# Norms of q and k in a decoder step: one square, one sum by head and one scaling per part, in two of three head groups

## The chip, the cores and the metric

The kernel runs on one core of a Trainium2 chip. The metric is the device time of one execution in microseconds (us), the median of three runs where several were made. A core has five engines that run at the same time, each working through its own list of instructions in order: TensorE (PE, with its weight loads shown as PEld) for matrix products, VectorE (DVE), ScalarE (ACT) and GpSimd (POOL) for elementwise work, and SyncE (SP), which issues transfers between device memory (DRAM) and the on-chip memory SBUF. PE writes its products to a small second memory, PSUM, from which DVE and ACT read. An instruction that needs another engine's result waits on a semaphore, and everything behind it on its own engine waits too.

## The reference, cut to what matters

One step of a decoder layer is computed for 1024 prompt tokens and 64 sample tokens (8 sequences of 8), width 1024. The part that the change touches is the norm of queries and keys: each of 12 heads of 64 channels, for q and for k, is divided by the root of its mean square over the token.

```python
def rms_norm(x, w):
    x32 = x.astype(F32)
    y = x32 * lax.rsqrt(jnp.mean(jnp.square(x32), axis=-1, keepdims=True) + EPS)
    return y.astype(x.dtype) * w

def project(x, ln1, w_in, q_norm, k_norm):
    p = jnp.einsum('btd,de->bte', rms_norm(x, ln1), w_in)
    a, q, k, v, g_a, g_b = jnp.split(p, IN_SPLITS, axis=-1)
    heads = lambda t: t.reshape(B, T, N_HEADS, HEAD_DIM)
    return a, rms_norm(heads(q), q_norm), rms_norm(heads(k), k_norm), heads(v), g_a, g_b
```

The heads form three groups of four. Each group attends over a window with its own stride: (128, 1), (512, 4), (2048, 16). The groups' outputs are combined by their softmax denominators, multiplied with gates and a pooling branch, and followed by an output projection and a feed-forward layer of width 4096. All of it is float32.

## The kernel before

**Order of the stages.** The pooling inputs come first (to about 60 us of the profiled execution), then the three head groups in the order 2, 1, 0 (to about 390 us, group 2 ending near 160), then the gates (tiles `pg`), the mixing and output projection (`pab`, `ph`), the feed-forward layer up (`pz`) and down (`pd`). Matrix products are made in three passes over high and low parts of both operands: `split` (lines 116 and 117) rounds a raw tile to its high part on ACT and subtracts to get the low part on DVE. The weights of q, k and v of one group lie in three rotating places (`places`), loaded through three raw buffers (`raw_qkv`) in pieces of 512 columns; SP issues a load when DVE's line 117 has freed a raw buffer.

**Parts.** In each group, `qkv_part` (line 605) runs for nine blocks of tokens: eight of 128 prompt tokens, and block 8 with the 64 sample tokens. For blocks 1 to 5, q and k are one part of 512 columns (a wide part, PSUM tile `pqk`) and v another of 256; for blocks 8, 0, 6 and 7, q, k and v are three parts of 256 (tiles `pq`, `pk`, `pv`; narrow parts). `js` lists what a part holds (0 for q, 1 for k, 2 for v) and is sorted by the place in which each weight lies. The places of q, k and v are 2, 0 and 1 in every group (`place[0]` is 2, 5 and 8 when a group takes them), so a wide part's `js` is [1, 0]: k in the first 256 columns of the tile, q in the others.

**The norm of one part.** After the matrix products of a q or k part, ACT squares each head's 64 columns from PSUM into the tile `qk` as scratch and accumulates their sum into one column of `ms` (line 642; the profile shows the square and an accumulator read). POOL adds epsilon (line 645) and raises to the power -1/2 (line 646, tile `mr`). Later, at the next step, `scale` multiplies each head's 64 columns from PSUM with its column of `mr` into `qk` on ACT (line 651). For a wide part these are 8 squares, 8 accumulator reads and 8 scalings.

**What follows a part.** Attention of a block is a generator that is advanced one step per part: PE transposes `qk` (line 667, tiles `tqg..`), ACT and DVE copy the result out (`qkT`, lines 669 and 670), PE makes scores (line 684, `sg..`), DVE adds the mask and takes the row extreme (line 693, `smg..` and `sta` or `md`), ACT takes exponentials (line 694), PE transposes them (line 703, `tpg..`), ACT copies that out (line 706, `pTg..`) and PE multiplies with v (line 717, `pog..`). Group 0 needs its tokens in natural order, so during a block's v part the next block's activations are cast into `natt` (line 601; the low halves on ACT, the high halves on DVE). The sample's own keys of group 2 run alongside groups 1 and 0: POOL multiplies loaded cache pieces (line 851, `pck` and `pcv`), DVE reduces or adds them (lines 864, 889, 890). `behind_pe` adds a wait on the most recent matrix product to an instruction; POOL's products of that loop also wait for the last norm on POOL (`last_norm`).

**Who sets the order.** PE's list is written out by hand: it runs in the order of the program. The lists of DVE, ACT, POOL and SP are ordered by a planner, which simulates the program with estimated durations and picks by priority whatever can start. The order is then fixed, whatever the real durations are.

Of the kernel before, what the change touches and what calls it, by code (L numbers as in the profile page):

```python
# [9 lines left out]
AF = mybir.ActivationFunctionType  # L10
ALU = mybir.AluOpType
AX = mybir.AxisListType
# [15 lines left out]
HD = 64  # L28
KPC = 4
H = TOK // 2  # L30
# [7 lines left out]
def decoder_step(ctx, tc, i, o):  # L38
    nc = tc.nc
    v_, s_, g_, t_ = nc.vector, nc.scalar, nc.gpsimd, nc.tensor  # L40
# [8 lines left out]
    def rr(p, shape, dt, name, tag, bufs):  # L49

        n = turn[p, tag] = turn.get((p, tag), -1) + 1
        return p.tile(shape, dt, name=name, tag=f"{tag}.{n % bufs}", bufs=1)
# [133 lines left out]
    def behind_pe(ins, mm=None):  # L186

        tc.add_manual_dep(ins.ins, (mm or last_mm[0]).ins.name,
                          mybir.DependencyInfo(mybir.DependencyClass.Sync, mybir.DependencyReason.DATA), reason="pace")

    def gemm(out, n_k, lhs, rhs, by_k=False, middle=None, quarter=None):

        if by_k == 2:
            terms = [(a, b, k) for k in range(n_k) for a, b in PASSES]
        elif by_k:
            terms = [(1, 0, k) for k in range(n_k)] + [(0, b, k) for k in range(n_k) for b in range(2)]
        else:
            terms = [(a, b, k) for a, b in PASSES for k in range(n_k)]
        for j, (a, b, k) in enumerate(terms):
            last_mm[0] = t_.matmul(out, lhs(a, k), rhs(b, k), start=(j == 0), stop=(j == len(terms) - 1))  # L200
            if middle and j == len(terms) // 2 - 1:
                middle()
            if quarter and j % 6 == 5:
                quarter(j // 6)
# [26 lines left out]
    def bank(name):  # L231
        held[0] = (held[0] + 1) % 4
        return acc_p.tile([P, 512], F32, name=name, tag=f"acc.{held[0]}", bufs=1)
# [212 lines left out]
    def soon(*fs):  # L446

        if fs:
            later.append(lambda: (fs[0](), soon(*fs[1:])))
# [108 lines left out]
    def step():  # L558
        for f in [later.pop(0) for _ in range(len(later))]:
            f()  # L560
        for r in list(active):
            if next(r, True):
                active.remove(r)
        cool[0] -= 1
        for r in waiting[:2]:
            if r not in primed:
                primed.add(r)
                next(r)
        if waiting and cool[0] <= 0:
            r = waiting.pop(0)  # L570
            if not next(r, True):
                active.append(r)
            cool[0] = 2
# [7 lines left out]
    def block_cols(g, blk, s, k):  # L581


        if g == 0:
            return nat[s, k]
        if g == 1:
            return act4[s][k][:, blk // 2, blk % 2 * P:(blk % 2 + 1) * P]
        return act4[s][k][:, blk // 2, blk % 2:2 * P:2]

    def res8(blk):  # L590
        return blk // 2 + 4 * (blk % 2)
# [4 lines left out]
    def in_order(blk, ks=range(0, KD, 2)):  # L596

        for s, copy in ((1, s_.copy), (0, v_.tensor_copy)):
            for k in ks:
                t = natt[:, 4 * s + k // 2]  # L600
                copy(t.rearrange("p k (l r) -> p k l r", r=4),
                     act_t[s].rearrange("p k (r l) -> p k l r", r=4)[:, k:k + 2, blk * 32:(blk + 1) * 32, :].bitcast(F32))
                nat[s, k], nat[s, k + 1] = t[:, 0, :], t[:, 1, :]

    def qkv_part(g, wts, blk, name, tiles, js, middle=None, quarter=None):


        n = min(P, TOK - blk * P)
        qk, vt = tiles
        go = 0 if blk == 8 else g  # L610
        col = res8(blk) if go == 2 else blk
        pt = bank(f"p{''.join('qkv'[j] for j in js)}{name}")
        js = sorted(js, key=lambda j: wts[j])
        N = 256 * len(js)
        at = places[:, wts[js[0]]:wts[js[-1]] + 1:max(1, wts[js[-1]] - wts[js[0]])]

        def rhs(s, k):
            return at[:, :, s, k * 256:(k + 1) * 256]

        if blk == 8:  # L620
            for k in range(KD):
                t_.matmul(pt[:, :N], smp_t[:, k, :], rhs(0, k), start=(k == 0), stop=(k == KD - 1))
                if k < KD - 1:
                    for kk in ((0, 1) if k == 0 else (k + 1,)):
                        last_mm[0] = t_.matmul(pt[:n, :N], smp_t[:, kk, :NS], rhs(1, kk), start=False, stop=False)
            v_.tensor_copy(vt[:n], pt[n:, :256])
            v_.tensor_tensor(pt[:n, :256], pt[:n, :256], vt[:n], op=ALU.add)
        else:
            by_k = 2 if quarter or js == [2] and (g == 0 or blk == 0) else g == 0
            gemm(pt[:n, :N], KD, lambda s, k: block_cols(g, blk, s, k), rhs, by_k, middle, quarter)  # L630
        for j in js:
            ends_of[g, blk, j] = last_mm[0]
        if blk < 8:
            if g == 0 and 2 in js and blk < 7:
                in_order(blk + 1)
        if js[0] < 2:
            ms = rr(ap1, [P, 8], F32, name=f"ms{name}_{js[0]}", tag="ms", bufs=4)
            r = rr(ap1, [P, 8], F32, name=f"mr{name}_{js[0]}", tag="mr", bufs=4)
            H = 4 * len(js)
            for u, j in enumerate(js):  # L640
                for h in range(4):
                    s_.activation(qk[:n, j * 256 + h * HD:j * 256 + (h + 1) * HD],
                                  pt[:n, u * 256 + h * HD:u * 256 + (h + 1) * HD], AF.Square,
                                  scale=HD ** -0.5, accum_out=ms[:n, 4 * u + h:4 * u + h + 1])
            g_.tensor_tensor(ms[:n, :H], ms[:n, :H], xeps[go][:n, col:col + 1].to_broadcast([n, H]), op=ALU.add)
            last_norm[0] = g_.tensor_tensor(r[:n, :H], ms[:n, :H], mhalf[:n, :H], op=ALU.pow)  # L646

            def scale():
                for u, j in enumerate(js):
                    for h in range(4):  # L650
                        behind_pe(s_.activation(qk[:n, j * 256 + h * HD:j * 256 + (h + 1) * HD],
                                                pt[:n, u * 256 + h * HD:u * 256 + (h + 1) * HD], AF.Copy,
                                                scale=r[:n, 4 * u + h:4 * u + h + 1]))
                    if j and blk == 8:
                        v_.tensor_tensor(qk[:n, 256:], qk[:n, 256:], wrow[:n], op=ALU.mult)
                        soon(lambda: sample_keys_out(g, qk))
        else:
            s_.activation(vt[:n], pt[:n, :256], AF.Copy, scale=rtok[go][:n, col:col + 1])
        step()
        if js[0] < 2:  # L660
            soon(scale)
# [446 lines left out]
    def sample_keys_out(g, qk):  # L1108
        rows, new = sample_rows_of(g)
        behind_pe(dma_st(rows[:, :256], qk[:64, 256:]))  # L1110
        if g == 2:
            behind_pe(dma_st(new[:, :512], qk[:64]))
# [23 lines left out]
    for g in (2, 1, 0):  # L1136
# [42 lines left out]
        for blks in ((8, 0), (1,), (2,), (3,), (4,), (5,)) + (((6, 7),) if g else ((6,), (7,))):  # L1179
# [12 lines left out]
            for js in (((0, 1), (2,)) if blks[0] in (1, 2, 3, 4, 5) else ((0,), (1,), (2,))):  # L1192
                for b in (blks[::-1] if g < 2 and js == (2,) and 8 in blks else blks):
# [13 lines left out]
                    if g == 1 and extra and (1, "keys") in done:  # L1207
                        extra = []
                        natt = np_.tile([P, 8, 2, P], F32R, name="natt", tag="nat")
                        soon(lambda: in_order(0, (0, 2)), lambda: in_order(0, (4, 6)))  # L1210
                    wide = len(js) == 2
                    qkv_part(g, wts, b, f"{g}_{b}", tiles[b], js, middle if wide else None,
                             quarter if g and b in (6, 7) else None)
                    feed()
# [139 lines left out]
    def row_tile(n, name):  # L1354
        return rr(rows_p, [P, H], F32, name=f"g{n}_{name}", tag=f"g{n}", bufs=2)
# [149 lines left out]
    for n, (f, a) in enumerate(order):  # L1505
# [5 lines left out]
        t = row_tile(1 + a, f)  # L1511
# [194 lines left out]
    for j in range(2):  # L1706
        for d in range(4):
# [4 lines left out]
            for m in range(2):  # L1712
# [19 lines left out]
                else:  # L1732
                    sq = rr(hq_p, [P, H], F32, name=f"hq{kk}_{j}", tag="hq", bufs=2)
# [478 lines left out]
```

## Time and profile before

| what | us |
|---|---|
| median of three runs (lowest, highest) | 1407.88 (1403.77, 1408.54) |
| profiled execution, its own time | 1405.47 |
| its span, first to last instruction | 1403.7 |
| DVE busy in the span | 965.2 |
| ACT busy in the span | 758.0 |
| POOL busy in the span | 234.2 |
| POOL's step `mr` (line 646), mean of 8 columns (15 times) | 1.77 |
| POOL's step `mr` (line 646), mean of 4 columns on 128 rows (18 times) | 1.11 |
| ACT's scaling of 64 columns from `pqk` (line 651), mean | 0.333 |
| ACT's square of 64 columns from `pqk` (line 642), mean | 0.232 |

All times are from one profiled execution except the first row. In the rows of the profile, the name before the arrow is the tile written, those behind it the tiles read; a shape is partitions by elements. In rows of a group, the number behind "x" counts instructions, then come busy time and mean duration in ns, then the idle time of that engine just before them with what ended most of it. In a timeline row the first two numbers are start and length in us, and the bracket holds the idle time before it and its releaser. In rows of waits, the three numbers are the total in us, how often, and the longest. A row of a stage gives its borders, its length and the busy time of PE, PEld, DVE, ACT and POOL, with the granted clock, the DMA share and GB/s last. The core's granted TensorE clock is 1.000 over the whole span.

### The profile page before, as it was taken

The numbers are of one execution on the slowest core, as the hardware profiler recorded it, in microseconds if no ns is written. First come the engines' busy times: TensorE is split into PE (matmuls) and PEld (weight loads), VectorE is DVE, ScalarE is ACT, GpSimd is POOL, SyncE is SP. The second block draws the span as 40 slices with busy tenths as digits, with TensorE's granted clock in tenths as the row PEclk, the third lists the DMA queues.
The fourth block names the chain that finished last, engine by engine and source line by source line (L and its number), as shares of the span: only waits on it lengthen the run. The fifth ranks groups of instructions, "written<-read, shape, count | busy, mean of one in ns | idle before, by whom it ended". The sixth has DMA issues, their size and how long they took to land.

```text
span 1403.7 us, 29517 instructions
## 1 busy us (share of the span) xinstructions
PE 1392.2 (99%) x11101; PEld 1343.0 (96%) x11101; DVE 965.2 (69%) x1766; ACT 758.0 (54%) x1962; POOL 234.2 (17%) x330
## 2 busy tenths in 40 slices
PE   9999999999999999999999999999999999999998
PEld 8988887888999999999999999999999999999998
DVE  7788775676676767876468677766665685665565
ACT  8557755777865323563336455554555544444443
POOL 0822265466500100000000000000000000000100
PEclk9999999999999999999999999999999999999999
DMA  6322788745477777975368668856758987777674
GB/s 215 117 88 101 223 219 221 205 132 146 113 254 228 246 230 243 320 233 183 127 200 285 228 221 269 269 200 211 253 186 290 321 275 261 234 240 232 205 259 169
DMA packets 184541, 303.58 MB, mean 216 GB/s; under 512 B 26567, under 2 KB 90509, under 8 KB 182350
## 3 DMA queue, kind: packets, MB, share of 16 engines
q1 hardware_dynamic: 181326, 258.04, 57.7%
q0 software_dynamic: 3072, 43.65, 9.8%
q8 instruction: 87, 1.43, 0.4%
q14 instruction: 56, 0.46, 0.1%
HBM read 231.55 MB, written 113.73 MB: 246 GB/s over the span
## 4 chain that ended last, share of the span: by engine, by line
PE 92%; DMA 3%; DVE 1%; ACT 1%; POOL 1%; issue 1%; SPq 0%; DVEq 0%; POOLq 0%; ACTq 0%
PE pz L1292 24%; PE pd L2070 24%; PE pg L1292 12%; PE ph L200 7%; PE pqk L200 5%; PE pab L1292 5%; PE pv L200 4%; PE a L328 3%; DMA raw_qkv<-in_w_in_dram 2%; PE pq L200 1%; PE pk L200 1%; PE sg0b L684 1%; PE pog0b L717 1%; PE tpg0b L703 0%; POOL mr L646 0%
## 5 line engine op out<-in xcount | busy, mean ns | idle before, releaser
L2070 PE MATMUL pd<-places 128*128 128x272 f32 x2688 | 331.8, 287 | 0.0
L2070 PEld LDWEIGHTS pd<-places 128*128 128x128 f32 x2688 | 331.6, 188 | 0.1
L116 ACT ACTIVATE places<-raw_d 128x544 fp32r<-128x544 f32 (+1 forms) x176 | 111.1, 647 | 161.8 <-DMA raw_d<-z_d 61.3
L117 DVE TENSOR_TENSOR places<-raw_d,places 128x544 fp32r<-128x544 f32 (+1 forms) x176 | 122.6, 711 | 92.3 <-ACT places L116 90.4
L2110 POOL DMA_DIRECT2D out_kv_sample_dram<-in_cache_kv_dram x96 | 47.1, 491 | 794.0 <-ACT places L116 582.9
L1292 PE MATMUL pz<-act,places 128*128 128x280 f32 (+1 forms) x1080 | 139.4, 287 | 0.0
L1292 PEld LDWEIGHTS pz<-act,places 128*128 128x128 f32 x1080 | 135.9, 188 | 0.0
L200 PE MATMUL ph<-act,places 128*128 128x280 f32 (+1 forms) x768 | 96.6, 287 | 0.0
L200 PEld LDWEIGHTS ph<-act,places 128*128 128x128 f32 x768 | 96.0, 188 | 0.1
L1292 PE MATMUL pg<-act,places 128*128 128x264 f32 (+1 forms) x576 | 75.6, 288 | 0.0
L1292 PEld LDWEIGHTS pg<-act,places 128*128 128x128 f32 x576 | 72.6, 188 | 0.6 <-issue 0.3
L1292 PE MATMUL pz<-places,apart 128*128 128x264 f32 (+1 forms) x528 | 67.9, 287 | 0.0
L1292 PEld LDWEIGHTS pz<-places,apart 128*128 128x128 f32 x528 | 66.6, 188 | 0.0
L200 PE MATMUL pqk<-places,act 128*128 128x512 f32 x240 | 60.5, 402 | 0.0
L1292 PE MATMUL pz<-act,apart 128*128 128x264 f32 (+1 forms) x456 | 59.1, 287 | 0.0
L1292 PEld LDWEIGHTS pz<-act,apart 128*128 128x128 f32 x456 | 57.5, 188 | 0.1
L200 PEld LDWEIGHTS pqk<-places,act 128*128 128x128 f32 x240 | 44.7, 192 | 9.6
L646 POOL TENSOR_TENSOR mr<-ms,mhalf 128x4 f32<-128x4 f32 (+2 forms) x39 | 52.8, 1354 | 3.1
L851 POOL TENSOR_TENSOR pck<-pck,qs 128x256 f32<-128x256 f32 x64 | 47.4, 774 | 28.6 <-DMA pck<-in_cache_kv_dram 12.4
L200 PE MATMUL pv<-places,act 128*128 128x256 f32 x384 | 50.2, 286 | 1.5 <-DVE places L117 1.5
L328 PE MATMUL a<-act,places 128*128 128x384 f32 (+1 forms) x288 | 50.5, 333 | 0.8 <-ACT act L306 0.8
L1292 PE MATMUL pab<-ab,places 128*128 128x264 f32 (+1 forms) x384 | 50.5, 287 | 0.0
(431 smaller groups left out, 2824.9 us busy)
## 6 DMA issues: line engine op xcount, KB each, us to landing
out_kv_sample_dram<-in_cache_kv_dram POOLq DMA_DIRECT2D x72, 480.0 KB, 5.2
raw_d<-z_d SPq DMA_DIRECT2D x112, 272.0 KB
z_d<-t SPq DMA_DIRECT2D x80, 272.0 KB
raw_d<-in_w_down_dram SPq DMA_DIRECT2D x80, 256.0 KB
raw_u<-in_w_up_dram SPq DMA_DIRECT2D x64, 256.0 KB
raw_qkv<-in_w_in_dram SPq DMA_DIRECT2D x36, 256.0 KB
pck<-in_cache_kv_dram SPq DMA_DIRECT2D x32, 256.0 KB
pcv<-in_cache_kv_dram SPq DMA_DIRECT2D x32, 256.0 KB
```

The costliest lines, as they stand in the source:

```text
L116: ins = s_.activation(dst_hi, src, AF.Copy)
L117: v_.tensor_tensor(dst_lo, src, dst_hi.bitcast(F32), op=ALU.subtract)
L200: last_mm[0] = t_.matmul(out, lhs(a, k), rhs(b, k), start=(j == 0), stop=(j == len(terms) - 1))
L328: last_mm[0] = t_.matmul(pts[m][:, :n], wt[:, a, kk, m * P:(m + 1) * P], act4[b][kk][:, :, part4(c)], start=(p == 0 and kk == 0), stop=(p ...
L646: last_norm[0] = g_.tensor_tensor(r[:n, :H], ms[:n, :H], mhalf[:n, :H], op=ALU.pow)
L684: t_.matmul(sc[e][:, hp, j * P:(j + 1) * P], qT[rows, hp, :], kT[rows, 2 + hp, :], start=True, stop=True)
L717: t_.matmul(po[e * HD:(e + 1) * HD, hp, :], vr[:, h * HD:(h + 1) * HD], pTs[e][:, hp * nk + j, :], start=(j == 0), stop=(j == nk - 1))
L851: ins = g_.tensor_tensor(out, *others, op=ALU.mult)
L1292: last_mm[0] = t_.matmul(out[c], lhs(*term), rhs(*term, c), start=(first and n == 0), stop=(n == len(terms) - 1), skip_group_check=not first)
L2070: last_mm[0] = t_.matmul(outs(chain[t], Q)[c], A[:, a, t * P:(t + 1) * P], Z[:, b, c], start=(fresh and f == 0 and n == 0), stop=(f == NG ...
L2110: ins = g_.dma_start(d, a)
```

## The change

In groups 1 and 0 the norm of a part is made from fewer and larger instructions. ACT squares all of the part's columns at once into the same scratch tile, without accumulating; DVE sums each head's 64 columns with one reduction into `ms`; POOL's two steps stay; and the scaling moves from ACT to DVE, as a product of the PSUM tile with the column of each head repeated over its 64 channels. If `js` is [0, 1] the scaling is one instruction over eight heads, else one per 256 columns. Group 2 keeps the form from before. For the narrow parts, the scratch is the part's own half of `qk`; for the wide ones it is the whole tile.

```diff
+    def by_head(t):
+        return t.rearrange("p (h d) -> p h d", d=HD)
+
     def qkv_part(g, wts, blk, name, tiles, js, middle=None, quarter=None):
...
             H = 4 * len(js)
-            for u, j in enumerate(js):
+            whole = g < 2
+            if whole:
+                sq = qk[:n, :N] if N == 512 else qk[:n, js[0] * 256:(js[0] + 1) * 256]
+                s_.activation(sq, pt[:n, :N], AF.Square, scale=HD ** -0.5)
+                v_.tensor_reduce(ms[:n, :H], by_head(sq), axis=AX.X, op=ALU.add)
+            for u, j in enumerate(js if not whole else []):
                 for h in range(4):
...
             def scale():
+                if whole:
+                    runs = [(0, 0, 8)] if js == [0, 1] else [(u, j, 4) for u, j in enumerate(js)]
+                    for u, j, m in runs:
+                        behind_pe(v_.tensor_tensor(by_head(qk[:n, j * 256:j * 256 + m * HD]), by_head(pt[:n, u * 256:u * 256 + m * HD]),
+                                                   r[:n, 4 * u:4 * u + m].unsqueeze(2).to_broadcast([n, m, HD]), op=ALU.mult))
                 for u, j in enumerate(js):
-                    for h in range(4):
+                    for h in range(0 if whole else 4):
                         behind_pe(s_.activation(qk[:n, j * 256 + h * HD:j * 256 + (h + 1) * HD],
                                                 pt[:n, u * 256 + h * HD:u * 256 + (h + 1) * HD], AF.Copy,
                                                 scale=r[:n, 4 * u + h:4 * u + h + 1]))
```

## The prediction

> **What bounds the kernel now.** I read the page first: TensorE is busy for 1392.2 of 1403.7 us, so only the other 11.5 us can be saved by anything that adds no matrix work. The sums by stage say where they lie (columns: us from the start, length, then busy us of PE, PE's weight loads, DVE, ACT, POOL), and PE's own waits say what ended them.
>
> ```profile
> PE 1392.2 (99%) x11101; PEld 1343.0 (96%) x11101; DVE 965.2 (69%) x1766; ACT 758.0 (54%) x1962; POOL 234.2 (17%) x330
> ...
> 0.00:60.00 60.00, 58.09 (x342) 56.19 (x343) 45.87 (x83) 44.95 (x71) 23.55 (x19) 1.00 0.53 172
> 60.00:160.00 100.00, 100.00 (x697) 88.35 (x696) 81.44 (x193) 67.68 (x345) 29.96 (x31) 1.00 0.35 114
> 160.00:300.00 140.00, 134.87 (x1156) 113.20 (x1155) 89.86 (x265) 90.80 (x440) 79.75 (x111) 1.00 0.76 208
> 300.00:390.00 90.00, 89.99 (x756) 78.11 (x755) 64.29 (x185) 72.70 (x311) 50.28 (x70) 1.00 0.53 144
> 390.00:1403.70 1013.70, 1009.27 (x8158) 1007.19 (x8156) 683.79 (x1042) 481.84 (x801) 50.69 (x100) 1.00 0.72 237
> ...
> PE pog1b L717 <- ACT pTg1b L706: 3.0, 3, 1.6
> PE pv L200 <- DVE places L117: 1.5, 1, 1.5
> PE sg1b L684 <- ACT pTg1b L706: 0.6, 1, 0.6
> ```
>
> The clock column is 1.00 in every stage. Groups 1 and 0 run from about 160 to 390 us; there PE lacks 140.00 - 134.87 + 0.01 = 5.1 us, and the three wait rows (total, times, longest) add up to the same 5.1: five waits, four of them for ACT's copies of the transposed scores, one for a weight half that DVE prepares. Everything else in 160 to 390 is PE at work. So the change can give back **at most 5.1 us, 0.36%**, of the profiled execution's 1405.47 us. That execution is 2.4 us below the median of the runs (1407.88), inside their spread of 4.8 us. A difference of about 0.5% (7 us) is what a measurement of this kernel can tell from no change.
>
> **What the change takes and adds.** ACT's and DVE's load first: the instructions on the normalized tile (its columns: PE, weight loads, DVE, ACT), and the rows that price the new ones.
>
> ```profile
> 160.00:300.00 140.00, 7.71 (x52) 5.49 (x52) 3.44 (x7) 39.01 (x264) 1.00 0.76 208
> 300.00:390.00 90.00, 4.49 (x28) 3.06 (x28) 0.42 (x1) 24.65 (x168) 1.00 0.53 144
> ...
> L706 ACT COPY pTg0b<-tpg0b 128x512 f32<-128x512 f32 x10 | 6.1, 614 | 1.9 <-PE tpg0b L703 1.9
> L706 ACT COPY pTg1b<-tpg1b 128x256 f32<-128x256 f32 x8 | 3.3, 408 | 2.7 <-PE tpg1b L703 2.7
> ...
> L864 DVE TENSOR_REDUCE sc<-pck 128x16 f32<-128x1024 f32 x16 | 19.5, 1219 | 14.8 <-POOL pck L851 8.4 <-PE pqk L200 3.1 <-PE pv L200 2.9
> ...
> 175.31 0.41 DVE L869 TENSOR_REDUCE sc<-ss 128x4 f32<-128x256 f32 x1
> ...
> L1009 DVE TENSOR_TENSOR od<-od,pos 128x256 f32<-128x256 f32 x6 | 2.5, 412 | 2.8 <-PE pos L1005 2.8
> ```
>
> Per group there are five wide parts (q and k together, 24 ACT instructions each: 8 squares, 8 accumulator reads, 8 scalings) and eight narrow ones (12 each): 2 x (5 x 24 + 8 x 12) = 432, the 264 + 168 of the rows. All 432 go, **63.7 us of ACT**. They come back as 26 squares: ten of 512 columns at 0.61 and sixteen of 256 at 0.41, priced by the copies out of PSUM of the same size: 12.7 us. ACT falls from 163.5 to 112.5 us in these 230.
>
> DVE gets 26 sums by head and 36 scalings. The wide parts keep two scalings of 256 columns, not one: the weight places are taken in the order 2, 0, 1, so the sorted pair is k, q and the single pass over eight heads is never reached. A sum over 512 columns lies between the rows of 256 (0.41) and 1024 (1.22): 0.68 at 1.05 ns a column. A scaling reads PSUM and a broadcast column as line 1009 reads PSUM: 0.41. Wide 10 x (0.68 + 0.82) = 15.0, narrow 16 x (0.41 + 0.41) = 13.1: **28.1 us more on DVE**, 154.2 to 182.3 of 230 (79%). A broadcast over the inner dimension has no row of its own with PSUM; its bounds are the 0.41 above and twice it, were the repeated column to halve the rate, 36 x 0.41 = 14.8 more; I take 0.41, as PSUM operands and elements are the same. DVE at 85% would still not be full.
>
> For one part, the latency between matmul and normalized tile falls too: by the rows below, four squares take 267.69 to 268.47, four scalings to 269.26, 1.6 us; a square of 0.41, a sum of 0.41 and a scaling of 0.41 take 1.2, and a wide part 2.0 instead of 3.2. POOL's two steps between stay, but now wait for DVE's sum; behind them in POOL's order stand the products of the sample's own keys, for which only DVE's reductions (line 864) wait. POOL is busy for 130 of the 230 us, so I price this at nothing; were that cover gone, the sample's end would be late, not PE's products here. No DMA is added, moved or made smaller, and the buffers are the same; but SP's weight loads wait for DVE to free raw buffers, so a late DVE also makes transfers late.
>
> **The five idle places, one by one.** First the largest (start, length, engine, line, idle before and who ended it):
>
> ```profile
> 267.14 0.64 ACT L116 ACTIVATE places<-raw_qkv 128x512 fp32r<-128x512 f32 x1 [1.45 <-DMA raw_qkv<-in_w_in_dram]
> 267.69 0.20 ACT L642 ACTIVATE qk<-pk 128x64 f32<-128x64 f32 x1
> ...
> 268.47 0.94 ACT L651 ACTIVATE qk<-pk,mr 128x64 f32<-128x64 f32 x4
> 269.26 0.67 ACT L601 CAST natt<-act 128x256 fp32r<-128x256 f32 x1
> 269.77 0.43 ACT L706 COPY pTg1b<-tpg1b 128x256 f32<-128x256 f32 x1
> ...
> 270.25 0.65 PE L717 MATMUL pog1b<-pTg1b,v 128*64 128x128 f32 x6 [1.62 <-ACT pTg1b L706]
> ```
>
> ACT stands on a weight DMA, then must pass squares, scalings and a cast before the copy that PE waits for. One square takes 0.31 to the next start (0.41 less the 0.1 by which neighbours overlap, 267.14 + 0.64 against 267.69) instead of 0.78, and the scalings' 0.79 go: the copy is about 1.26 earlier, and **1.62 shrinks to about 0.35, -1.3**. The DMA is now what is late.
>
> ```profile
> 205.00 1.75 ACT L651 ACTIVATE qk<-pqk,mr 128x64 f32<-128x64 f32 x8 [1.90 <-POOL mr L646]
> 207.07 0.65 PE L717 MATMUL pog1b<-pTg1b,v 128*64 128x128 f32 x6 [0.42 <-ACT pTg1b L706]
> 219.62 1.75 ACT L651 ACTIVATE qk<-pqk,mr 128x64 f32<-128x64 f32 x8 [3.22 <-POOL mr L646]
> 221.90 0.71 PE L684 MATMUL sg1b<-qkTg1b 64*128 64x128 f32 x6 [0.57 <-ACT pTg1b L706]
> ...
> 295.36 0.93 ACT L651 ACTIVATE qk<-pk,mr 128x64 f32<-128x64 f32 x4 [1.18 <-POOL mr L646]
> 297.15 0.38 ACT L706 COPY pTg1b<-tpg1b 128x256 f32<-128x256 f32 x1
> 297.58 0.65 PE L717 MATMUL pog1b<-pTg1b,v 128*64 128x128 f32 x6 [0.98 <-ACT pTg1b L706]
> ```
>
> In the first two, ACT waits for POOL's power and scales eight heads while the copy is queued behind; without the scalings both go: **-0.4 and -0.6**. The third has the same form, but two exponentials stand in front of the copy, and they need DVE's masked scores:
>
> ```profile
> 295.11 0.41 DVE L693 CUSTOM_DVE_ANT_0 smg1b<-sg1b,cst 128x256 f32<-128x256 f32 x1
> ...
> 295.45 0.42 DVE L693 CUSTOM_DVE_ANT_0 smg1b<-sg1b,cst 128x256 f32<-128x256 f32 x1
> ...
> 171.75 0.43 DVE L857 SCALAR_TENSOR_TENSOR qs<-wq,qs 128x256 f32<-128x256 f32 x1 [3.11 <-PE pk L200]
> 174.51 0.87 DVE L117 TENSOR_TENSOR places<-raw_qkv,places 128x512 fp32r<-128x512 f32 x1
> 175.44 0.74 PE L200 MATMUL pv<-places,act 128*128 128x256 f32 x4 [1.54 <-DVE places L117]
> ```
>
> If DVE's masking comes before the new scaling, the copy is 0.8 earlier; if the scaling, which cannot start before POOL's power at about 295.3, comes first, masking is 0.5 to 0.6 later and the wait grows by 0.2. I take **-0.4**. The fifth is DVE's own: after 3.11 us of idleness it works off a queue that ends in the weight half at 174.51. Nothing leaves this queue and up to two scalings (0.8) may join it; half of that, **+0.4**. For new waits behind DVE elsewhere I take +0.3. Sum: -1.3 - 0.4 - 0.6 - 0.4 + 0.4 + 0.3 = **-2.0 us**, or 1403.5 on the profiled execution and 1405.9 on the median; I forecast **1405**, between the two and nearer the median, since a result is a median. Bounds: -5.1 if every wait goes, and above zero the slower rival.
>
> [...]
>
> **The rivals.** *Nothing on the path changes* (20%): ACT's copies are released by something else as late, such as the DMA of 267.14; what DVE delays gives back what ACT saves. 1407, within 0.5%. For it speaks that only 5.1 us are in play.
>
> *The waits for POOL move to DVE* (14%, slower). ACT's waits and the place with the least slack behind DVE:
>
> ```profile
> ACT qk L651 <- POOL mr L646: 14.7, 9, 3.7
> ...
> 213.31 0.49 ACT L694 ACTIVATE smg1b<-smg1b,sta 128x256 f32<-128x256 f32 x1
> 216.27 0.66 PE L703 MATMUL tpg1b<-cst,smg1b 128*128 128x128 f32 x4
> ...
> 354.39 1.64 POOL L646 TENSOR_TENSOR mr<-ms,mhalf 128x8 f32<-128x8 f32 x1
> 356.17 1.02 DVE L601 CAST natt<-act 128x256 fp32r<-128x256 f32 x3
> 357.08 1.18 PE L200 MATMUL pq<-places,natt 128*128 128x256 f32 x8
> ```
>
> ACT stood 14.7 us in nine waits before its scalings. DVE runs in order; a scaling set before POOL is ready holds masks, casts and weight halves behind it, and PE and SP wait for these. The casts of the next block end at 357.19, when PE has begun on that block at 357.08: a scaling pair (0.82) in front would reach PE nearly whole, in seven block changes of group 0 up to 5.7 us; of the nine waits the two of 3.7 and 3.2 exceed the 2.5 us that PE leaves the masks elsewhere (the last exponential ends at 213.80, PE turns its tile at 216.27) and add 1.9. 1407.88 + 7.6 = **1415.5**. It decides from the point where scalings precede the casts in most blocks. POOL's power ends at 356.0, just before these casts, so either order is open; against it speaks that DVE is idle for a third of 160 to 390. [...]
>
> *All stalls go* (10%, faster): the 2.4 us by which the median exceeds the profile are waits of the same kind, and DVE costs nothing: 1407.88 - 5.1 - 2.4 = **1400.4**.
>
> **How the numbers follow.** The forecast has 56%, with 1405 and alone about 1401 to 1409. Range 1399 to 1414: the low end is the lowest run, 1403.77, less 5.1; the high end stops just short of the slower rival. Faster by over 0.5% (under 1400.8) 10%, slower (over 1414.9) 14%, within 76%.
>
> **What would show it.** Right: ACT's busy time in 160 to 390 near 112 us, DVE's near 182; PE's waits for line 706 near 0.5 us instead of 3.6; a wait of POOL's power under DVE, in the new scaling line. Wrong: PE waits for casts, masks or weight halves of DVE that sum to over 3 us; a scaling row near 0.8 us; a lack of PE after 390 above the 4.4 us of now (1013.70 - 1009.27).

## The result, and the profile after

The changed kernel takes **1410.95 us** in the median of 22 runs (1408.51 to 1412.78), the kernel before 1407.65 us in 22 runs beside it (1402.74 to 1413.10). The ratio is **1.0021 (1.0011 to 1.0031)**: slower by about 3 us. That is less than the 0.5% set as a limit ahead of time, but the interval lies wholly above 1, and the sign is not the one forecast. The profiled execution took 1409.76 us (span 1408.0) against 1405.47 (1403.7) before, 4.3 us more, so its rows show a little more than the medians' difference.

The page's busy times after:

```profile
PE 1393.8 (99%) x11101; PEld 1343.9 (95%) x11101; DVE 987.0 (70%) x1828; ACT 709.5 (50%) x1556; POOL 236.1 (17%) x330
```

The stages (PE, PEld, DVE, ACT, POOL, clock, DMA, GB/s):

```profile
0.00:60.00 60.00, 57.11 (x340) 55.31 (x341) 45.61 (x83) 45.28 (x71) 23.52 (x19) 1.00 0.53 172
...
160.00:300.00 140.00, 135.97 (x1158) 114.45 (x1157) 103.81 (x305) 61.88 (x193) 80.25 (x110) 0.99 0.78 208
300.00:390.00 90.00, 87.47 (x718) 74.94 (x719) 69.94 (x197) 51.63 (x140) 52.28 (x70) 1.00 0.48 127
390.00:1408.00 1018.00, 1013.23 (x8196) 1010.77 (x8194) 686.71 (x1056) 483.62 (x812) 50.63 (x100) 1.00 0.73 237
```

And the instructions on the normalized tile alone (PE, PEld, DVE, ACT):

```profile
160.00:300.00 140.00, 7.72 (x52) 5.50 (x52) 21.10 (x46) 7.32 (x17) 0.99 0.78 208
300.00:390.00 90.00, 3.83 (x24) 2.64 (x24) 10.91 (x24) 4.39 (x9) 1.00 0.48 127
```

The work moved as described: on this tile ACT falls from 63.7 to 11.7 us and DVE rises from 3.9 to 32.0. But PE's lack in 160 to 390 us is 4.03 + 2.53 = 6.6 us where it was 5.1, and the clock column shows 0.99 in a stage that had 1.00. PE's waits in these 230 us (total, times, longest):

```profile
PE pog1b L730 <- ACT pTg1b L719: 2.1, 1, 2.1
PE tps L991 <- ACT p L985: 2.0, 1, 2.0
PE sg1b L697 <- DVE keys L980: 0.7, 1, 0.7
PE pqk L200 <- DVE qk L660: 0.5, 1, 0.5
PE pv L625 <- DVE qk L660: 0.3, 1, 0.3
PE pss L978 <- DMA kt<-in_kT_dram: 0.3, 1, 0.3
PE sg1b L697 <- DVE p L980: 0.3, 1, 0.3
PE pq L200 <- DVE natt L601: 0.2, 1, 0.2
```

Three of the five waits of before are gone (at 207, 222 and 298 us), and so is the one for the weight half at 175. The one at 270 us grew from 1.62 to 2.13. The one of 2.0 us at 316 us is new, and so are five small ones behind DVE and one behind a transfer. The 4.3 us are made up of: 1.4 from PE's larger lack (6.56 against 5.14); about 1.5 from 3.41 us at half the clock, which began at 270.95 (24 products of `pv` took 4.59 us there instead of 3.10; last section); 0.3 after 390 (4.77 against 4.43); and 1.0 before 60 us, where the code is unchanged.

The new wait of 2.0 us can be followed upstream. The kernel before, around the same place, DVE and then ACT (start, length):

```profile
306.32 2.13 DVE L601 CAST natt<-act 128x256 fp32r<-128x256 f32 x4
...
309.43 0.69 DVE L890 TENSOR_TENSOR ss<-ss,pcv 128x512 f32<-128x512 f32 x1
310.04 0.29 DVE L967 TENSOR_TENSOR p<-pss,cst 128x136 f32<-128x136 f32 x1
```

```profile
309.69 1.75 ACT L651 ACTIVATE qk<-pqk,mr 128x64 f32<-128x64 f32 x8 [2.24 <-POOL mr L646]
```

ACT waited 2.24 us for POOL's power there, and DVE went on past it. The changed kernel: POOL, DVE, ACT and PE.

```profile
306.97 2.63 POOL L864 TENSOR_TENSOR pcv<-pcv,sc 128x256 f32<-128x256 f32 x4 [3.40 <-DMA pcv<-in_cache_kv_dram]
309.56 0.35 POOL L653 TENSOR_TENSOR ms<-ms,stats 128x8 f32<-128x8 f32 x1
309.99 1.67 POOL L654 TENSOR_TENSOR mr<-ms,mhalf 128x8 f32<-128x8 f32 x1
```

```profile
310.43 0.68 DVE L902 TENSOR_TENSOR pcv<-pcv 128x512 f32<-128x512 f32 x1
311.69 0.76 DVE L660 TENSOR_TENSOR qk<-pqk,mr 128x256 f32<-128x256 f32 x2 [0.59 <-POOL mr L654]
312.36 1.10 DVE L903 TENSOR_TENSOR ss<-ss,pcv 128x512 f32<-128x512 f32 x1
313.39 0.29 DVE L980 TENSOR_TENSOR p<-pss,cst 128x136 f32<-128x136 f32 x1
...
314.18 0.23 DVE L706 CUSTOM_DVE_ANT_0 smg0b<-sg0b,cst 128x128 f32<-128x128 f32 x1
```

```profile
314.45 0.40 ACT L707 ACTIVATE smg0b<-smg0b,md 128x128 f32<-128x128 f32 x1 [6.88 <-DVE md L706]
...
315.62 0.39 ACT L985 ACTIVATE p<-p,obs 128x136 f32<-128x136 f32 x1
```

```profile
316.16 0.33 PE L991 MATMUL tps<-cst,p 128*128 128x128 f32 x1 [1.96 <-ACT p L985]
```

POOL's power ends at 311.66 and the scaling starts at 311.69. Behind it in DVE's order stand an addition, `p` (the masked scores of the sample, 3.35 us later than before: 313.39 against 310.04) and the masks. The wait for POOL is only 0.59 of these 3.35 us. Start to start, the scaling pair takes 0.67, the new sum by head ahead of the casts 0.59, and the addition and the casts 0.4 each more than before; DVE came to this place 0.7 late. ACT stands 6.88 us until the first mask is there, and PE waits for ACT's exponential of `p`. That exponential needs `obs`, the row extreme of `p` on DVE, and the planner has put `obs` behind three of the four masks (314.76) and the exponential behind three of ACT's; before, both stood ahead of all four (`obs` at 310.84, the first mask at 310.99). The scaling's waits for POOL sum to 6.6 us on DVE in 160 to 390 (10 times, longest 1.8); that is the wait that ACT had before (14.7 in nine), on an engine that has more behind it.

### The profile page after: what moved, and what is told of

The parts are those of the page before. It is cut to its first block, busy times and chain, and to the rows that moved or that the text cites. A ratio compares the mean times of both kernels' runs of the same rounds, so it can differ in the third digit from the quotient of the medians.

```text
span 1408.0 us, 29215 instructions
## 1 busy us (share of the span) xinstructions
PE 1393.8 (99%) x11101; PEld 1343.9 (95%) x11101; DVE 987.0 (70%) x1828; ACT 709.5 (50%) x1556; POOL 236.1 (17%) x330
## 4 chain that ended last, share of the span: by engine, by line
PE 86%; DMA 6%; POOL 2%; DVE 2%; ACT 1%; SPq 1%; issue 1%; DVEq 0%; POOLq 0%; ACTq 0%
PE pz L1305 23%; PE pd L2083 22%; PE pg L1305 12%; PE ph L200 7%; PE pab L1305 5%; PE pqk L200 3%; PE a L328 3%; PE pv L200 3%; DMA raw_qkv<-in_w_in_dram 2%; PE pq L200 1%; DMA pck<-in_cache_kv_dram 1%; POOL pcv L864 1%; DMA raw_d<-in_w_down_dram 1%; POOL mr L654 1%; PE pk L200 1%
## 5 line engine op out<-in xcount | busy, mean ns | idle before, releaser
L328 PEld LDWEIGHTS a<-act,places 128*128 128x128 f32 x288 | 47.9, 188 | 3.6 <-ACT act L306 1.6
```

The costliest lines, as they stand in the source:

```text
L328: last_mm[0] = t_.matmul(pts[m][:, :n], wt[:, a, kk, m * P:(m + 1) * P], act4[b][kk][:, :, part4(c)], start=(p == 0 and kk == 0), stop=(p ...
```

## The experiments

Three theories. **A**: the scaling on DVE waits for POOL's power and holds masks, products and casts behind it. **B**: DVE's added 28 us cost as such, wherever they lie. **C**: with other instructions the planner orders everything anew, and casts and copies far from the scaling come to stand badly. All ratios are to the kernel before, run in turn on the same chip (medians of 1406.51 to 1407.65 us). They are given as recorded and are not the quotients of the medians, from which they differ by up to 0.0015 (e16: 1408.01 beside 1406.51 for the kernel before).

| run | median us | ratio (95%) | PE's waits at 300 to 325 us, longest |
|---|---|---|---|
| changed, first | 1410.95 | 1.0021 (1.0011 to 1.0031) | ACT L985, 2.0 |
| e13, changed again | 1410.74 | 1.0012 (0.9999 to 1.0025) | ACT L985, 2.6 |
| e1, sum only | 1408.53 | 1.0009 (0.9993 to 1.0024) | PE pog1b, 1.0 |
| e2, scaling only | 1411.92 | 1.0030 (1.0016 to 1.0043) | DVE sta, 0.6 |
| e4, group 1 only | 1407.90 | 1.0007 (0.9993 to 1.0022) | DVE sta, 0.6 |
| e5, group 0 only | 1411.52 | 1.0029 (1.0015 to 1.0042) | ACT L985, 2.4 |
| e3, no wait for the power | 1405.54 | 0.9989 (0.9979 to 1.0000) | DVE pxs, 0.8 |
| e8, group 0 scaled a step later | 1406.87 | 0.9993 (0.9978 to 1.0008) | DVE pxs, 0.2 |
| e9, first natt casts later | 1410.27 | 1.0019 (1.0007 to 1.0031) | ACT L985, 2.1 |
| e10, both later | 1406.75 | 0.9988 (0.9975 to 1.0002) | none |
| e11, as e8 without block 8 | 1408.38 | 1.0001 (0.9986 to 1.0016) | DVE pxs, 1.3 |
| e12, as e11, group 1 too | 1407.61 | 1.0000 (0.9983 to 1.0016) | DVE pxs, 0.8 |
| e15, block 1 alone later | 1408.28 | 1.0010 (0.9996 to 1.0023) | DVE pxs, 0.6 |
| e16, blocks 1 to 5 later | 1408.01 | 0.9996 (0.9982 to 1.0010) | DVE pxs, 0.8 |
| e17, blocks 2 to 5 later | 1411.29 | 1.0028 (1.0013 to 1.0044) | ACT L985, 3.1 |

**Halves of the change: e1 and e2.** e1 makes squares and sums the new way and scales on ACT by head; e2 squares and accumulates as before and scales on DVE.

```diff
 e1, in scale():
-                if whole:
+                if False:
...
-                    for h in range(0 if whole else 4):
+                    for h in range(4):
 e2, ahead of POOL's steps:
-            if whole:
+            if False:
...
-            for u, j in enumerate(js if not whole else []):
+            for u, j in enumerate(js):
```

> Groups 1 and 0: one square per part on ACT and the sum by head on DVE, but the scaling stays on ACT by head. Theory A (the scaling on DVE costs: it waits for POOL's power in DVE's list and holds masks and casts behind it): ratio to before 0.998 to 1.000, PE's waits behind DVE in 300 to 390 us under 0.5 us, no wait like the one of 2.0 us at 316. Theory B (DVE's added time as such costs; the sums are 13.4 of its 28 us): ratio 1.001, half of the loss. Theory C (the planner's new order of ACT and DVE sets it, whatever moves): ratio anywhere from 0.998 to 1.003, with PE's long waits at places that neither A nor B names.

> Groups 1 and 0: squares and sums by head on ACT as before, the scaling on DVE. Theory A: the whole loss stays, ratio 1.002 or more, waits of DVE's scaling for POOL's power of 6 us or more in all. Theory B: half of the loss, 1.001. Theory C: 0.998 to 1.003, with other places.

The sum alone costs nothing that can be told from zero, though its 1.0009 is what B forecast and lies above A's range; the scaling alone costs as much as the whole change, so the scaling it is. But e2's profile does not have the wait at 316 us. DVE has the same order there as in the changed kernel, and the scaling waits 0.59 us again (it starts at 315.66), but PE comes to this place later: its 24 products of `pqk` begin 1.13 us before the scaling (314.53), in the changed kernel 3.36 before it (308.33). Its largest lack is at 274.5 us, 3.3 us for the copy of `pTg1b`, and the records show half the clock for 3.41 us from 177.3 and for 6.83 us from 272.8 (the granted clock of 160 to 300 us is 0.96). In that profile the time lost earlier covers this wait. Why that copy is so late in e2 was not followed up.

**Halves of the groups: e4 and e5.**

```diff
-            whole = g < 2
+            whole = g == 1        (e4)      whole = g == 0        (e5)
```

> The whole change in group 1 alone. From the two profiles PE's loss in group 1 (160 to 300 us) is small: waits of 1.7, 0.6 and 1.2 us go, about 1.6 at 176 to 180, 0.4 at 207 and 0.5 at 270 come, and a clock dip of 1.4 us follows the wait at 270. Theories A and B: ratio 0.999 to 1.000. Theory C: 0.998 to 1.003.

> The whole change in group 0 alone. In the profile of the changed kernel PE loses 2.1 us at 316, 0.45 at 333 and 0.9 at 361 there, which before had no wait: theories A and B: ratio 1.0015 to 1.0025, with these waits. Theory C: 0.998 to 1.003, with other places.

Group 0 makes the loss; group 1's share is within what can be told from zero. Both ratios are a little above what was expected. e5's profile has the wait at 316 us (2.4 us), but not the two smaller ones that were expected at 333 and 361.

**The wait itself: e3.** Same instructions on the same engines, but the scaling reads the sum instead of the power.

```diff
+            if whole:
+                g_.tensor_tensor(r[:n, :H], ms[:n, :H], xeps[go][:n, col:col + 1].to_broadcast([n, H]), op=ALU.add)
+                last_norm[0] = g_.tensor_tensor(r[:n, :H], r[:n, :H], mhalf[:n, :H], op=ALU.pow)
...
-                                                   r[:n, 4 * u:4 * u + m].unsqueeze(2).to_broadcast([n, m, HD]), op=ALU.mult))
+                                                   ms[:n, 4 * u:4 * u + m].unsqueeze(2).to_broadcast([n, m, HD]), op=ALU.mult))
```

> As after, but the scaling on DVE is by the sum of squares itself, not by POOL's power of it: POOL still makes its two steps, nobody waits for them. Epsilon and power are so left out of the norms of groups 1 and 0. Theory A (the scaling waits for POOL with masks and casts behind it): DVE's waits for POOL at L654 (6.6 us in 160-390 us of after) are gone, TensorE's wait for ACT at 316 us falls from 2.0 to at most 1.3 us, and the ratio to before falls from 1.0021 to 1.000-1.001. Theory B (DVE's added time as such): DVE is as busy as in after (173.8 us in 160-390), so the ratio stays at about 1.002. Theory C (the planner's order of casts and copies): the waits at 270 us (2.1 us) and after 176 us stay, so the ratio falls by no more than 0.0005.

B is ruled out, and e3 is faster still than A expected (1.000 to 1.001): 1405.54 us, 5 us below the changed kernel, at an unchanged load of DVE (102.88 + 69.97 = 172.9 us in 160 to 390 against 173.8). In e3's DVE timeline the scaling of 311.69 starts when DVE comes to it, and `p` follows at 310.31 instead of 313.39:

```profile
309.05 0.74 DVE L664 TENSOR_TENSOR qk<-pqk,ms 128x256 f32<-128x256 f32 x2
309.71 0.68 DVE L906 TENSOR_TENSOR pcv<-pcv 128x512 f32<-128x512 f32 x1
310.31 0.29 DVE L984 TENSOR_TENSOR p<-pss,cst 128x136 f32<-128x136 f32 x1
```

The planner's order is not the same, however: the addition now stands behind `p`, and `obs` ahead of the masks. So e3 shows that the load is not the cause; it does not take out the wait alone.

**The same wait moved, not removed: e8, e9, e10.** e8 gives out group 0's scaling one step later in the program, e9 does so with the first `natt` casts, four of which stand ahead of the copy that PE waits for at 270 us; e10 does both. In e8, e10, e11 and e12 the prompt keys of group 0's last block are stored before they are scaled (in e12 group 1's too); the rest is the full computation.

```diff
-            soon(scale)
+            soon(*([lambda: None] if g == 0 else []), scale)                               (e8, e10)
...
-                        soon(lambda: in_order(0, (0, 2)), lambda: in_order(0, (4, 6)))
+                        soon(lambda: None, lambda: in_order(0, (0, 2)), lambda: in_order(0, (4, 6)))   (e9, e10)
```

> As after, but in group 0 the scaling is given out one step later in the program, when POOL has had more time. Theory A: DVE's waits for POOL in 300-390 us go, the wait at 316 us falls from 2.0 to under 1 us, ratio to before 1.000-1.001, as long as the transposes that read the scaled tile don't come to wait for it instead (then a wait of TensorE on DVE L660 of 0.5-1.5 us stands there, and the ratio stays at 1.002). Theory B: ratio about 1.002. Theory C: a changed order moves other waits too, the sum by under 1 us either way.

> As after, but the first casts of group 0's natt tiles are given out one step later. Theory C (at 270 us four such casts stand on ACT ahead of the copy of pT for which TensorE waits 2.1 us, after which the records show half the clock for 3.4 us): the wait falls to under 0.6 us and the half clock behind it goes, so -2 to -3.5 us of after, ratio 0.9995-1.001. Theory A: this has nothing to do with the scaling, the wait at 316 us (2.0 us) stays, ratio not below 1.000. Theory B: ratio stays at 1.002.

> Both moves: the scaling of group 0 and the first natt casts each one step later. Theories A and C together: the waits at 270 us (2.1) and 316 us (2.0) and the half clock behind the first go, so about -4 to -5 us of after, 1404-1406 us, ratio 0.998-0.9995, faster than before. Theory B: DVE is as busy as in after, ratio 1.002.

e8 does what A expected, with a ratio a little lower. e9 is a miss: it does not change the order at the place it was made for. ACT still takes four casts and then the copy:

```profile
269.48 2.23 ACT L601 CAST natt<-act 128x256 fp32r<-128x256 f32 x4
271.60 0.38 ACT L719 COPY pTg1b<-tpg1b 128x256 f32<-128x256 f32 x1
```

So e9 does not decide about C; it shows that a move in the program need not change the planner's order where one wants it. How much the wait at 270 us adds to the median stays open. e10 came to 1406.75, a little above its 1404 to 1406, and cannot be told from e8.

**How wide the move must be: e11 and e12, and both kernels again: e13 and e14.**

```diff
+            soon(*([lambda: None] if g == 0 and blk < 8 else []), scale)     (e11; e12: g < 2)
```

> As after, with the scaling of group 0 one step later for blocks 0 to 7 alone; the sample block (block 8) has it where after has it. Theory A (a scaling given out before POOL is ready holds masks and casts on DVE behind it): as with the later scaling of all of group 0, no wait of TensorE for ACT L985 at 316 us, waits of the scaling for POOL in 160-390 us down from 6.6 to about 3-4 us (group 1's are left), median 1406-1407.5 us, ratio 0.998-1.000, below after's 1.0021 by at least 0.001. Theory B (DVE's added time as such): 1.002.

> As after, with the scaling one step later in group 1 too (blocks 0 to 7 of groups 1 and 0). Theory A alone: the last waits of the scaling for POOL go as well (under 1 us of 160-390), and the ratio is that of the later scaling in group 0 or up to 0.0007 below it (0.998-0.9995). Against it: the tile of products then leaves its PSUM bank a step later in 160-300 us as well, where TensorE already waits for the scaling at 179 us (pqk L200 <- DVE qk L660, 0.5 us); if that wait grows by over 1 us in all, the ratio is 0.0005-0.0015 above that of the later scaling in group 0 alone. Theory B: 1.002.

> The changed kernel once more, unchanged, for a second profile and more times beside the others. Theory A: the waits of DVE's scaling for POOL (6.6 us, 10 times) and TensorE's wait for ACT L985 at 316 us (2.0 us) stand again, ratio 1.001-1.003. If the wait at 316 us is under 1 us here with the same time, it is chance of one execution and not the cause. The half clock after the wait at 271 us is expected again only if that wait is again about 2 us.

> The kernel before once more, for a second profile. All theories: no wait of TensorE for ACT near 314-316 us above 1 us, the waits for the pT copy (about 3.0 us in 3) as in the first profile, no stretch of half clock in 160-390 us; span 1403-1407 us. If a 2 us wait and half clock stand here too, the differences between single profiles are chance, and the times alone decide.

e11 and e12 lie at the kernel before, both just above what was expected; moving group 1 as well gains nothing that shows. The changed kernel again has the wait at 316 us, with half the clock behind it this time, and not behind the wait at 271 us, though that is 2.0 us again. Its ratio of 1.0012 (0.9999 to 1.0025) reaches 1, so alone it would not show a loss. The kernel before again (1406.50 us in the median of 8) has no such wait and no half clock in 160 to 390:

```profile
PE tps L991 <- ACT p L985: 2.6, 1, 2.6
```

```profile
PE pog1b L717 <- ACT pTg1b L706: 2.3, 3, 1.0
PE pv L200 <- DVE places L117: 1.8, 1, 1.8
```

The first row is e13's, the other two are all that e14 has.

**Which scaling: e15, e16, e17.** The wait of 2.0 us or more at 316 us stood behind one scaling, that of group 0's block 1. e15 moves it alone, e17 the four that follow, e16 all five. All compute the full result.

```diff
-            soon(scale)
+            soon(*([lambda: None] if (g, blk) == (0, 1) else []), scale)           (e15)
+            soon(*([lambda: None] if g == 0 and 0 < blk < 6 else []), scale)       (e16)
+            soon(*([lambda: None] if g == 0 and 1 < blk < 6 else []), scale)       (e17)
```

> As after, with one scaling alone (group 0, block 1, the one at 311.7 us) one step later. If that scaling makes the loss: TensorE's wait for ACT L985 at 316 us falls from 2.0-2.6 us to at most 0.8, the median is 1407-1409 us, ratio 1.000-1.001. If the loss is spread over all scalings of group 0: the wait at 316 us goes too, but at least half of the loss stays, ratio 1.001-1.002. If the wait comes back in another place: ratio 1.002.

> As after, with the scaling of the wide parts of group 0 (blocks 1 to 5) one step later. Theory A: no wait for ACT L985 above 0.8 us at 316 us, the scaling's waits for POOL in 300-390 us under 1 us (3.5 in after); median 1406-1408.5 us, ratio 0.9990-1.0005, so it is faster than after and at best equal to before within what can be measured. Theory B (DVE's added time as such): 1.002.

> As after, with the scalings of group 0's blocks 2 to 5 one step later and that of block 1 where after has it. If the one scaling of block 1 makes the loss: the wait at 316 us stays at 2.0-2.6 us and the ratio at 1.0015-1.0025. If it is spread: ratio 1.0005-1.001, in spite of the wait at 316 us.

With block 1's scaling at its first place (e17) the whole loss is there, 1.0028; with that one scaling moved as well (e16) it is gone, 0.9996: **3.3 us (1411.29 - 1408.01) for the place of one pair of instructions**, the intervals apart. e17's wait and ratio are a little above what was expected. e15 lies between, at 1.0010, as expected, and its interval reaches both. The same stretch of DVE in e17 and in e16:

```profile
311.50 0.76 DVE L660 TENSOR_TENSOR qk<-pqk,mr 128x256 f32<-128x256 f32 x2 [1.53 <-POOL mr L654]
312.17 1.10 DVE L903 TENSOR_TENSOR ss<-ss,pcv 128x512 f32<-128x512 f32 x1
313.19 0.29 DVE L980 TENSOR_TENSOR p<-pss,cst 128x136 f32<-128x136 f32 x1
...
314.56 0.28 DVE L984 TENSOR_REDUCE obs<-p 128x1 f32<-128x136 f32 x1
```

```profile
312.00 0.69 DVE L903 TENSOR_TENSOR ss<-ss,pcv 128x512 f32<-128x512 f32 x1
312.61 0.29 DVE L980 TENSOR_TENSOR p<-pss,cst 128x136 f32<-128x136 f32 x1
...
313.19 0.23 DVE L984 TENSOR_REDUCE obs<-p 128x1 f32<-128x136 f32 x1
...
315.74 0.75 DVE L660 TENSOR_TENSOR qk<-pqk,mr 128x256 f32<-128x256 f32 x2
```

In e16 POOL's power ended at 312.85 (311.16 + 1.69), later than in e17 (311.46), and DVE did not wait for it at all, for it had the addition, `p`, `obs`, the masks and some copies to do first. The orders of ACT, DVE and POOL in the two runs differ at this place alone, but not in the pair alone: in e16 the planner also put `obs` ahead of the masks, two small copies ahead of some of them, and ACT's exponential of `p` ahead of those of the masks. That exponential starts 0.85 us after `p` in e16 and 2.23 after it in e17. So the place of the scaling makes the loss, as shown, by the scaling itself, its wait and what the planner rearranges close around it; no run separates these. Of PE's time, 14.43 us pass in e17 from the start of its 24 products of `pqk` (307.03) to the next `pqk`, and 10.83 in e16. The difference of 3.6 us is for the most part the longer wait (3.06 against 0.75) and about 1.5 us of half clock behind it (last section).

e16 has the lowest ratio of the forms tried that keep the whole change and compute all of the result; it cannot be told from the kernel before and does not beat it.

The same pattern stands in group 1, where the size of the wait varies with DVE's order unchanged. At 207 us a scaling and a reduction of 1.21 us stand ahead of `p`; PE's wait there is 0.31 us in the changed kernel's first profile, 0.61 in e13's, and 1.80 in e16's (DVE, then PE). Why it varies was not followed up.

```profile
206.72 0.76 DVE L660 TENSOR_TENSOR qk<-pqk,mr 128x256 f32<-128x256 f32 x2 [1.24 <-POOL mr L654]
207.39 1.21 DVE L877 TENSOR_REDUCE sc<-pck 128x16 f32<-128x1024 f32 x1
```

```profile
209.21 0.49 PE L697 MATMUL sg1b<-qkTg1b,qkTg1b 64*128 64x128 f32 x4 [1.80 <-DVE p L980]
```

## Why the prediction was wrong

**The load of the engines was right.** ACT in 160 to 390 was forecast at 112 us and is 61.88 + 51.63 = 113.5. The new instructions on DVE were priced at 28.1 us; the tile's DVE time rose by 32.0 - 3.9 = 28.1. A scaling with a broadcast column takes 0.42 us (median), so the upper bound of twice that was not needed. DVE's busy time as a whole rose by 19.6 only, to 173.8 against a forecast of 182: the copies into `qS` took 9.7 us instead of 13.4, some work moved behind 390 us, and rows overlap their neighbours by some 0.1 us. The load as such makes no loss: e3 has the same load and none.

**Three of the five places were right.** The waits for the copy of `pTg1b` at 207, 222 and 298 us went, as forecast (-0.4, -0.6, -0.4; the last gave 1.0). That for the weight half at 175 was forecast at +0.4 and went too: here DVE's new order was better than expected.

**The place at 270 us was wrong** (-1.3 forecast, +0.5 measured). The sum took the scalings and squares off ACT and kept the rest of ACT's list. The planner put four casts where one had been:

```profile
267.65 0.36 ACT L646 ACTIVATE qk<-pk 128x256 f32<-128x256 f32 x1
267.92 2.19 ACT L601 CAST natt<-act 128x256 fp32r<-128x256 f32 x4
270.01 0.37 ACT L719 COPY pTg1b<-tpg1b 128x256 f32<-128x256 f32 x1
```

The 1.3 us freed on ACT were filled by 1.5 us of casts (2.19 against 0.67).

**The step that failed is the last term of the sum**, "For new waits behind DVE elsewhere I take +0.3". In the profile PE's new waits that go back to the scaling or stand directly behind DVE sum to 2.0 + 0.7 + 0.5 + 0.3 + 0.3 + 0.2 = 4.0 us, and the experiments put most of the loss on the largest of them: e17 less e16 is 3.3 us, the half clock behind the wait included. With 4.0 in place of 0.3, the sum's -2.0 would have been +1.7. The five places together gave -3.0 where -2.3 was forecast, so this term alone turned the sign; that the error at 270 us was more than made up at 175 and 298 is luck. The sum also had no term for the clock, which took about another 1.5 us in that profile.

**The rival that came true was named and priced too high.** "The waits for POOL move to DVE" had the mechanism in the main: a scaling set before POOL is ready holds what is behind it. It did not have the planner's new order around it. Its price was 7.6 us, from casts at seven block changes and two long waits; the measured price is about 3 us, most of it from one block, through `p` and the masks. So its chance of 14% was attached to a slowing of over 0.5%, and a smaller slowing by the same cause had no case of its own. The argument against it, that DVE is idle for a third of the time, does not bear on it: what counts is what stands behind the scaling at that moment. The trace had the sign of it: ACT's wait of 2.24 us for POOL at 309.69, with DVE's `p` at 310.04 beside it, is in the profile of before, and the prediction did not price that place.

The rows from 310.43 on show DVE keeping its order: the addition of line 903 needs the product of line 902, which ends at 311.11, and nothing of the scaling; DVE stands idle for 0.59 us, and the addition begins at 312.36, behind the scaling.

## What to carry to other kernels

Before work with a wait in front of it is moved from one in-order engine to another, list for each of these waits what will stand behind it on the new engine and who needs that soonest; one bad place can cost more than all the waits that are saved. An instruction that waits for a slow engine (here POOL, 1.67 us for its power) belongs behind the work that others wait for, and one step later in the program was enough here (e16). Where a planner orders the lists, an edit moves instructions far from it, so a gain at one place is only an estimate until its new neighbours are known.

## What the hardware showed unexpectedly

Behind some waits of PE the records show half the clock for 3.41 us, at a price of about 1.5 us: behind 2.13 us in the changed kernel's first profile (from 270.95), behind 2.61 in e13 (from 317.70) and behind 3.06 in e17 (from 317.07). In e17, the record and the stretches of 3.41 us before and after it (the clock is the third number from the end):

```profile
313.66:317.07 3.41, 1.12 (x9) 1.03 (x10) 3.17 (x18) 2.80 (x12) 0.65 (x2) 1.00 0.63 168
317.07:320.48 3.41, 3.41 (x18) 3.41 (x17) 2.73 (x7) 2.01 (x5) 2.54 (x4) 0.50 0.69 184
320.48:323.89 3.41, 3.41 (x22) 2.96 (x21) 2.07 (x4) 1.94 (x4) 3.25 (x5) 1.00 0.70 155
```

The price shows in the 24 products of `pv` that follow, first in e17 and then in the kernel before, 4.60 against 3.06 us:

```profile
316.89 4.60 PE L200 MATMUL pv<-places,natt 128*128 128x256 f32 x24
```

```profile
314.57 3.06 PE L200 MATMUL pv<-places,natt 128*128 128x256 f32 x24
```

The first profile of the changed kernel had the same kind of wait at 316 us, 1.96 us long, and kept its clock; the 24 products of `pv` behind it took 3.06 us (from 317.10):

```profile
312.80:316.20 3.40, 1.44 (x8) 0.83 (x6) 3.18 (x18) 1.75 (x9) 1.71 (x3) 1.00 0.36 92
316.20:319.60 3.40, 3.40 (x29) 3.31 (x30) 3.37 (x9) 3.12 (x9) 1.38 (x3) 1.00 0.61 161
```

In e11 too the clock stayed at 1.00, behind a wait of 2.5 us:

```profile
268.80:272.20 3.40, 0.86 (x8) 0.49 (x8) 2.78 (x6) 3.40 (x8) 2.31 (x3) 1.00 0.94 215
272.20:275.60 3.40, 3.40 (x31) 3.23 (x32) 3.40 (x14) 2.94 (x10) 1.32 (x2) 1.00 0.20 60
```

Eleven of the profiles have records of half the clock between 160 and 390 us, thirteen in all, of 3.41 us (eleven) or 6.83 us (two, in e2 and e4). The length of the wait does not tell whether one follows: behind 1.80 us in e16 (ended at 209.21) the clock was 0.51 from 211.00 to 214.40, behind the 2.5 us in e11 and 2.0 us in e13 at 271 us it stayed at 1.00. Nor does PE's busy time in the 3.4 us around the wait: 0.86 us in e11 left the clock as it was, 1.12 us in e17 did not. What decides was not shown, nor why two of the records are twice as long.
